# A two-layer encoder step on one core: in the RWKV-7 layer, values projected with tokens on the partitions, and a scan whose state is summed in PSUM and written by ScalarE

## The chip, the cores and the metric

One core of a Trainium2 chip runs the whole program. The metric is device time in microseconds (us), here of three runs, and of one more execution under the hardware profiler. The engines are TensorE (PE), VectorE (DVE), ScalarE (ACT), GpSimd (POOL) and SyncE (SP, which issues the DMAs).

## The reference

Two layers, each `x + Mixer(RMSNorm(x))`, on 2048 prompt tokens and 8 x 16 sample tokens of 1024 channels. Layer 1 is a gated DeltaNet; the change is in layer 2, RWKV-7, with 16 heads of 64 channels:

```python
rkvz = einsum('gbtd,dge->gbte', xs[:4], w_in)          # r, k, v, z: 1024 -> 4 x 1024
kk = l2_normalize(k * k_k);  k = k * (1 + (a - 1) * k_a)
def step(S, inp):                                       # S: one 64 x 64 state for each head
    sa = einsum('bhvk,bhk->bhv', S, a_t)
    S = S * w_t + sa * b_t + v_t * k_t
    return S, einsum('bhvk,bhk->bhv', S, r_t)
S, o = lax.scan(step, s0, (r, decay, k, v, -kk, kk * a))
o = group_norm(o) * gn_w + gn_b                         # by head
o = o + sum(r * k * r_k) * v                            # the bonus
y = (o * silu(z)) @ w_out
```

## The kernel before

The 2176 tokens of layer 2 run in six blocks: the first has two prompt chunks of 64 tokens and the 128 sample tokens (256 columns), the other five have six prompt chunks (384 columns). In a block the channels run in eight pairs of heads, q = 0..7, 128 channels each, so there are 48 steps of some 40 us. A step weaves, in twelve rounds, six stages of six successive pairs (`b_prep`, `b_subst`, `b_inverse`, the scan, `b_gate`, `b_out`) with 17 pieces of the projections of what comes next (`b_stream`). The order of TensorE is the written one; on the other engines and in SP's DMA queue a scheduler sorts by due times, DMAs with a lead of their own.

- **Projections** (`b_stream`, L1062 to L1064): 128x128 weights stationary, the mixed tokens `xh`, `xl` (high and low halves, made by `b_lerp` and L162/L163) moving with 384 columns, three matmuls for a product: 48 for a pair and group. `b_keep` copies the result with channels on the partitions to `kvo` (ACT) and writes it to DRAM (`kvd`); `b_load` reads K, R and V back.
- **`b_prep`**: products on POOL (L1181) and DVE; norm sums `pn`, twelve one-column matmuls (L1188); the bonus, one matmul with a block of ones over `rk` (L1198) into `pbn`, multiplied by V on DVE (L1200); Gram matrices (L1211), `N` (L1225, one half on DVE, one on POOL), then by DMA through DRAM `scrb` (L1236) into `B` (L1238).
- **`b_subst`**: a chain of small DVE operations L844/L846 on `B`, then by DMA into `cm`.
- **`b_inverse`**: POOL spreads `cm` into `T` (L1268), TensorE inverts by blocks (L1284 on), and twelve transposes (L106) turn V, which ACT copies into `XV` (L1327).
- **The scan**: a chunk is two rounds. First `px` (L1382) from `XV`, two ACT copies (L1385, L1386) and `Sw` = decay x state on ACT (L1384). In the second round KR·S (L1389) and TM·XV (L1393, into `pu`), then three DVE operations: the next chunk's `XV` twice (L1395) and the state `R` (L1396), each `pu` x decay + `Sw`; then L1398. There are 256 chunks in all.
- **`b_gate`, `b_out`**: normalise, turn back (L106), two fused DVE operations (L1485 and the next line) for weight, bonus, bias and gate, split into `oh`, `ol` (L163), output projection (L168 to L170).

A write of `whl` (L125) splits raw weights; `whl<-wd` loads split ones again. The functions that the change touches:

Of the kernel before, what the change touches and what calls it, by code (L numbers as in the profile page):

```python
# [29 lines left out]
NCI, NXH, NOH, NKO = 2, 8, 2, 2  # L30
# [41 lines left out]
class _K:  # L72
# [829 lines left out]
    def b_setup_side(self):  # L902

        nc, io, bp = self.nc, self.io, self.sp
        self.nacc, self.weng = 3, nc.vector
# [123 lines left out]
    def b_stream(self, blocks):  # L1029
# [17 lines left out]
        for b, units in pairs:  # L1047
            NT, first = b["NT"], units[0]
            if first == (1, 0):
                b["kv"] = self.dram.tile([4, KT, P, NT], F32, name=self.nm("kvd"), tag="kvd", bufs=2)  # L1050
# [4 lines left out]
            for s in range(4):
                for j, (g, q) in enumerate(units):
                    wh, wl = next(W)
                    o = p[j][:, 0:NT]
                    for i in range(2):
# [5 lines left out]
                    if s == 3:  # L1065
                        self.b_keep(b, g, q, p[j])
# [4 lines left out]
                    yield  # L1071

# [31 lines left out]
    def b_prep(self, b, q):  # L1104
# [88 lines left out]
        nc.vector.tensor_scalar(m2[:, 1, 0:nq], m2[:, 0, 0:nq], -1.0, None, op0=MUL)  # L1193
        yield
# [35 lines left out]
        d.update(KR=KR, BK=BK, m2=m2, bv=bv, GM=GM, N=N)  # L1230
# [24 lines left out]
    def b_inverse(self, b, q):  # L1255
# [3 lines left out]
        N, BK, V, GM = d["N"], d["BK"], d["V"], d["GM"]  # L1259
# [97 lines left out]
    def b_scan(self, b, q):  # L1357
# [19 lines left out]
        for c in range(ncp):  # L1377
# [5 lines left out]
            Sw = self.lp.tile([P, 64], F32, name=self.nm("Sw"), tag="Sw", bufs=2)  # L1383
            nc.scalar.activation(Sw, S, AF.Copy, scale=wc)  # L1384
# [78 lines left out]
    def b_gate(self, b, q):  # L1463
# [12 lines left out]
        nc.gpsimd.tensor_tensor(OC, OC, g[:, 0, 0:nq].unsqueeze(2).to_broadcast([P, nq, 64]), op=MUL)  # L1476
        yield
# [49 lines left out]
def _prep(inp):  # L1527
# [34 lines left out]
    o["b_prm"] = prm  # L1562
    w2 = np.stack([f["b_w_w2"][0], f["b_a_w2"][0]]).reshape(2, 64, KT, P).transpose(2, 1, 0, 3)
# [108 lines left out]
```

## Time and profile before

| what | value |
|---|---|
| median of three runs | 4623.11 us (4621.35 to 4625.97) |
| profiled execution | 4610.68 us, span 4608.9 us |
| busy in the span | PE 4299.8 (93%), DVE 3470.3 (75%), ACT 2287.8 (50%), POOL 1749.9 (38%) us |
| mean granted clock of TensorE | 0.966 |
| DMA | 842.18 MB, 183 GB/s |

Layer 2 begins near 2420 us of the span. Busy time is the union of an engine's instructions; a row of a timeline gives start and length, and in brackets the idle time ahead of it and what ended that. The granted clock is a share of full speed, 0.50 being the lower of the two levels. Times of the steps below are against the profiled execution, which stands 12.4 us (0.27%) under the median of the runs.

### The profile page before, as it was taken

To read this page: it belongs to the slowest core of one execution; us is meant where nothing else is said; L and a number is where in the kernel's file an instruction comes from. 1 tells how busy PE (TensorE), PEld (TensorE's weight loads), DVE (VectorE), ACT (ScalarE), POOL (GpSimd) and SP (SyncE) were. 2 spreads that over 40 slices of the span, in tenths; PEclk is the share of its full clock that TensorE was granted. 3 is DMA by queue.
4 is the path that set the end of the run, shared out by engine and by line. 5 is a ranking of instruction groups with operands and counts; after the bars stand their busy time and mean duration, and the time that the engine had idled before them with its cause. 6 is when DMAs were issued, how large, how long until landed. Compare 5 with 4: busy or idle time off the path is not lost. (4 is left out here: it accounts for less than half of the span.)

```text
span 4608.9 us, 104071 instructions
## 1 busy us (share of the span) xinstructions
PE 4299.8 (93%) x37093; PEld 3697.1 (80%) x37093; DVE 3470.3 (75%) x9203; ACT 2287.8 (50%) x6132; POOL 1749.9 (38%) x2507
## 2 busy tenths in 40 slices
PE   7999999999999999999987889999999999999996
PEld 6888788888888899999986767778787887887775
DVE  7888776676666776766677888877778778777885
ACT  5554454454344434444466665655455446446543
POOL 7666543322111211112103555445444434344441
PEclk9999999999999999999998989999999999999997
DMA  6666665556445576666655667766675665665542
GB/s 192 210 202 207 211 208 172 174 187 192 142 140 159 174 212 186 183 213 188 179 159 175 206 196 229 223 179 196 191 203 166 197 206 163 201 195 146 145 129 72
DMA packets 765670, 842.18 MB, mean 183 GB/s; under 512 B 263480, under 2 KB 497360, under 8 KB 765152
## 3 DMA queue, kind: packets, MB, share of 16 engines
q1 hardware_dynamic: 765152, 835.53, 59.9%
q8 instruction: 294, 4.82, 0.4%
q14 instruction: 224, 1.84, 0.1%
HBM read 632.73 MB, written 202.53 MB: 181 GB/s over the span
## 5 line engine op out<-in xcount | busy, mean ns | idle before, releaser
L453 PE MATMUL ps<-hh,whl 128*128 128x384 f32 (+1 forms) x1960 | 795.3, 406 | 12.8 <-ACT hh L162 10.6
L455 PE MATMUL ps<-hh,whl 128*128 128x384 f32 (+1 forms) x1960 | 711.8, 363 | 6.9 <-POOL whl L125 6.7
L454 PE MATMUL ps<-hl,whl 128*128 128x384 f32 (+1 forms) x1960 | 710.9, 363 | 1.7 <-DVE hl L163 1.4
L1062 PE MATMUL ps<-xh,whl 128*128 128x384 f32 (+1 forms) x1632 | 605.3, 371 | 32.0 <-ACT xh L162 17.4
L1063 PE MATMUL ps<-xl,whl 128*128 128x384 f32 (+1 forms) x1632 | 557.8, 342 | 22.0 <-POOL xl L163 11.2
L1064 PE MATMUL ps<-xh,whl 128*128 128x384 f32 (+1 forms) x1632 | 556.8, 341 | 9.2 <-DVE whl L125 8.8
L125 POOL TENSOR_TENSOR whl<-wraw,whl 128x256 fp32r<-128x256 f32 x454 | 374.6, 830 | 358.6 <-ACT whl L124 331.5
L573 DVE SCALAR_TENSOR_TENSOR cv<-pre,cw,cv 128x512 f32<-128x512 f32 (+3 forms) x576 | 375.3, 660 | 134.9 <-ACT cv L571 130.2
L453 PEld LDWEIGHTS ps<-hh,whl 128*128 128x128 f32 x1960 | 371.9, 190 | 65.8 <-issue 14.1
L168 PE MATMUL ps<-oh,whl 128*128 128x384 f32 (+2 forms) x1024 | 390.3, 381 | 26.6 <-DMA whl<-wd 13.9
L124 ACT CAST whl<-wraw 128x256 fp32r<-128x256 f32 x726 | 287.2, 402 | 255.5 <-DMA wraw<-in_w_b 74.3
L455 PEld LDWEIGHTS ps<-hh,whl 128*128 128x128 f32 x1960 | 371.4, 189 | 48.2 <-POOL whl L125 12.7
L454 PEld LDWEIGHTS ps<-hl,whl 128*128 128x128 f32 x1960 | 372.7, 190 | 34.0 <-DVE hl L163 4.6
L1062 PEld LDWEIGHTS ps<-xh,whl 128*128 128x128 f32 x1632 | 320.7, 197 | 75.3 <-ACT xh L162 23.0
L169 PE MATMUL ps<-ol,whl 128*128 128x384 f32 (+2 forms) x1024 | 366.8, 358 | 7.6 <-DVE ol L163 7.6
L844 DVE TENSOR_TENSOR sbt<-B,TB 48x15 f32<-48x15 f32 (+14 forms) x1320 | 351.9, 267 | 22.3 <-DMA B<-scr 1.7
L170 PE MATMUL ps<-oh,whl 128*128 128x384 f32 (+2 forms) x1024 | 363.6, 355 | 1.8 <-POOL whl L125 1.8
L846 DVE TENSOR_TENSOR TB<-TB,sbt 48x15 f32<-48x15 f32 (+14 forms) x1320 | 348.9, 264 | 19.8
L1063 PEld LDWEIGHTS ps<-xl,whl 128*128 128x128 f32 x1632 | 322.5, 198 | 33.8 <-POOL xl L163 17.2
L1064 PEld LDWEIGHTS ps<-xh,whl 128*128 128x128 f32 x1632 | 321.7, 197 | 16.8 <-DVE whl L125 16.2
L822 DVE TENSOR_TENSOR x<-x,ps 128x384 f32<-128x384 f32 (+1 forms) x320 | 191.1, 597 | 79.4 <-PE ps L170 77.9
L168 PEld LDWEIGHTS ps<-oh,whl 128*128 128x128 f32 x1024 | 196.6, 192 | 66.1 <-ACT oh L162 10.7
(349 smaller groups left out, 10233.7 us busy)
## 6 DMA issues: line engine op xcount, KB each, us to landing
whl<-wd SPq DMA_DIRECT2D x1582, 256.0 KB
wd<-whl SPq DMA_DIRECT2D x428, 256.0 KB
wraw<-in_w_a SPq DMA_DIRECT2D x288, 128.0 KB
wraw<-in_w_b SPq DMA_DIRECT2D x256, 128.0 KB
kvd<-kvo SPq DMA_DIRECT2D x160, 192.0 KB
xn<-x1d SPq DMA_DIRECT2D x80, 192.0 KB
wraw<-in_w_ao SPq DMA_DIRECT2D x96, 128.0 KB
xn<-in_x SPq DMA_DIRECT2D x32, 256.0 KB
```

What stands on the lines that cost most here:

```text
L125: (self.nc.gpsimd if tag == "o" else self.weng).tensor_tensor(w[:, 1], raw, w[:, 0].bitcast(F32), op=SUB)
L168: self.nc.tensor.matmul(out, lhsT=wh, rhs=hh, start=first and i == 0, stop=False)
L169: self.nc.tensor.matmul(out, lhsT=wh, rhs=hl, start=False, stop=False)
L170: self.nc.tensor.matmul(out, lhsT=wl, rhs=hh, start=False, stop=i == n - 1)
L453: nc.tensor.matmul(p, lhsT=wh[:, k % 2], rhs=hh, start=k == 0, stop=False)
L454: nc.tensor.matmul(p, lhsT=wh[:, k % 2], rhs=hl, start=False, stop=False)
L455: nc.tensor.matmul(p, lhsT=wl[:, k % 2], rhs=hh, start=False, stop=k == KT - 1)
L573: nc.vector.scalar_tensor_tensor(o, f(j), self.cw[:, ct, j:j + 1], o, op0=MUL, op1=ADD)
L844: nc.vector.tensor_tensor(o, B[:, j + 1:16, j:j + 1].to_broadcast([rows, m, j + 1]), T[:, j:j + 1, 0:j + 1].to_broadcast([rows, m, j + 1]) ...
L1062: nc.tensor.matmul(o, lhsT=wh[:, i], rhs=xh, start=k == 0, stop=False)
L1063: nc.tensor.matmul(o, lhsT=wh[:, i], rhs=xl, start=False, stop=False)
L1064: nc.tensor.matmul(o, lhsT=wl[:, i], rhs=xh, start=False, stop=k == KT - 1)
```

## The change

Three things in layer 2. **Values with tokens on the partitions:** `b_values` makes the tokens stationary (128 at a time, L1093 to L1095 of the new code) and moves 256 columns of weights, for two pairs at once; a matmul with a zero operand opens the bank that two token tiles share (L1090). `b_keep_values` makes three ACT copies for two pairs, and `XV` is loaded by DMA in `b_inverse` (L1316), so V isn't loaded, turned or copied. **The bonus by token:** the sum of `rk` is twelve one-column matmuls (L1225) right behind `pn`, two rounds earlier than the old matmul; POOL makes `bv` = `XV` x sum (L1364), and the gate adds it ahead of the turn, with the norm's weight from a broadcast tile. **The scan:** the state enters `pu` by a matmul with the identity (L1430), so `pu` x decay is the new state; ACT writes it (L1435 twice, L1436), and `Sw` goes.

```diff
-NCI, NXH, NOH, NKO = 2, 8, 2, 2
+NCI, NXH, NOH, NKO = 2, 8, 2, 3
...
+                    if g == 2:
+                        self.b_values(b, 2 * s + j, wh, wl, p)
+                        if s == 3 and j:
+                            self.b_keep_values(b, first[1], p)
...
+        if k == 0:
+            self.nc.tensor.matmul(p[0], lhsT=self.zero.to_broadcast([P, P]), rhs=wh.unsqueeze(1).to_broadcast([P, 2, 256]), start=True, stop=False)
+        for t in range(b["NT"] // P):
+            o, ts = p[t // 2][:, t % 2 * 256:t % 2 * 256 + 256], slice(t * P, (t + 1) * P)
+            self.nc.tensor.matmul(o, lhsT=xh[:, ts], rhs=wh, start=k == 0 and t == 2, stop=False)
...
+        for t in range(b["NT"] // P):
+            v = self.sp.tile([P, 256], F32, name=self.nm("kvo"), tag="kvo", bufs=NKO)
+            self.nc.scalar.copy(v, p[t // 2][:, t % 2 * 256:t % 2 * 256 + 256])
+            self.nc.sync.dma_start(b["vt"][t * P:(t + 1) * P, q * P:q * P + 256], v)
...
+        pb = self.ps("g")
+        for c in range(nq):
+            for h, hs in enumerate(HS):
+                nc.tensor.matmul(pb[HS[1 - h], c:c + 1], lhsT=c3(rk)[hs, c], rhs=self.ones[hs, 0:1], start=True, stop=True,
+                                 tile_position=(64 * h, 64 - 64 * h))
...
-        pbn = self.ps("g")
-        nc.tensor.matmul(pbn[:, 0:NT], lhsT=cb[:, B_BO:B_BO + P], rhs=rk, start=True, stop=True)
-        bv = self.lp.tile([P, NT], F32, name=self.nm("bv"), tag="bv", bufs=4)
-        nc.vector.tensor_tensor(bv, pbn[:, 0:NT], V, op=MUL)
+        bs = self.mp.tile([P, 8], F32, name=self.nm("bs"), tag="bs", bufs=3)
+        nc.scalar.activation(bs[:, 0:nq], pb[:, 0:nq], AF.Copy, scale=0.5)
...
+            nc.sync.dma_start(XV[os, 0:nq, h], vt[:, :, vs])
...
-        pt = self.ps("g")
-        for c in range(nq):
-            for h, hs in enumerate(HS):
-                self.turn(pt[HS[1 - h], c * 64:(c + 1) * 64], c3(V)[hs, c], h, 1 - h)
...
-            nc.scalar.copy(XV[os, 0:nq, h], c3(pt[os, 0:nq * 64]))
+            nc.gpsimd.tensor_tensor(bv[os], XV[os, 0:nq, h], d["bs"][os, 0:nq].unsqueeze(2).to_broadcast([64, nq, 64]), op=MUL)
...
-            Sw = self.lp.tile([P, 64], F32, name=self.nm("Sw"), tag="Sw", bufs=2)
-            nc.scalar.activation(Sw, S, AF.Copy, scale=wc)
...
+                nc.tensor.matmul(pu[HS[h], 0:64], lhsT=self.ident[HS[h], HS[h]], rhs=S[HS[h]], start=True, stop=False,
+                                 tile_position=(64 * h, 64 * h))
...
-                nc.vector.scalar_tensor_tensor(XV[HS[h], c + 1, h], pu[HS[h], 0:64], wc[HS[h]], Sw[HS[h]], op0=MUL, op1=ADD)
-            nc.vector.scalar_tensor_tensor(S, pu[:, 0:64], wc, Sw, op0=MUL, op1=ADD)
+                nc.scalar.activation(XV[HS[h], c + 1, h], pu[HS[h], 0:64], AF.Copy, scale=wc[HS[h]])
+            nc.scalar.activation(S, pu[:, 0:64], AF.Copy, scale=wc)
...
+        nc.vector.tensor_tensor(OC, OC, self.gw[:, q:q + 1].to_broadcast([P, nq, 64]), op=MUL)
+        nc.vector.tensor_tensor(OC, OC, d["bv"], op=ADD)
...
-        nc.vector.scalar_tensor_tensor(og, pu[:, 0:NT], self.hp[:, q, 3:4], og, op0=MUL, op1=ADD)
-        nc.vector.scalar_tensor_tensor(og, og, self.hp[:, q, 4:5], SZ, op0=ADD, op1=MUL)
+        nc.vector.scalar_tensor_tensor(og, pu[:, 0:NT], self.hp[:, q, 4:5], SZ, op0=ADD, op1=MUL)
```

**TensorE, a step in a six-chunk block, before:** the second half of a scan chunk, projections, the matmul of the bonus, and `px` of the next chunk. A name is a buffer with its number; `x2` are the two heads.

```order
L1389 MATMUL ps_46696<-R_30377,KR_44648 64x64 x2
L1393 MATMUL ps_46994<-XV_45920,TM_45919 64x64 x2
L1398 MATMUL ps_46696<-XV_45920,GM_45017 64x64 x2
L1062 MATMUL ps_46756<-xh_46431,whl_46835 128x384
L1063 MATMUL ps_46756<-xl_46432,whl_46835 128x384
L1064 MATMUL ps_46756<-xh_46431,whl_46835 128x384
L1062 MATMUL ps_46756<-xh_46438,whl_46835 128x384
L1063 MATMUL ps_46756<-xl_46439,whl_46835 128x384
L1064 MATMUL ps_46756<-xh_46438,whl_46835 128x384
L1198 MATMUL ps_47013<-ch_46784,cb 128x384
L1382 MATMUL ps_47023<-XV_45920,GM_45017 64x64 x2
```

After, the second half of a chunk:

```order
L1425 MATMUL ps_46159<-R_30380,KR_44236 64x64 x2
L1430 MATMUL ps_46870<-R_30380,ident 64x64 x2
L1433 MATMUL ps_46870<-XV_45490,TM_45489 64x64 x2
L1438 MATMUL ps_46159<-XV_45490,GM_44572 64x64 x2
L168 MATMUL ps_46885<-oh_45814,whl_46837 128x384
```

and the place where `pn` stands in a step of a block of the same kind, between two pieces of the values:

```order
L1093 MATMUL ps_47049<-whl_46912,xh_46568 128x256
L1094 MATMUL ps_47049<-whl_46912,xl_46569 128x256
L1095 MATMUL ps_47049<-whl_46912,xh_46568 128x256
L1219 MATMUL ps_47195<-ones,ch_47078 64x1 x12
L1225 MATMUL ps_47208<-ones,ch_47080 64x1 x12
L1420 MATMUL ps_47236<-XV_46120,GM_45279 64x64 x2
L1093 MATMUL ps_47048<-whl_46989,xh_46679 128x256
```

The bonus matmul is gone from the place ahead of `px`, its twelve small ones stand behind `pn`, and the identity's pair stands between KR·S and TM·XV.

**ScalarE, before, around one chunk:** `Sw`, a cast of mixed tokens, `XV` of the next pair, and the two copies of `px`.

```order
L1101 CAST w_11335_45847<-w2r_45845 128x256
L1384 ACTIVATE Sw_44815<-R_30371,wc_42563 128x64
L162 CAST xh_44626<-xt_44623 128x384
L1327 COPY XV_44575<-ps_44791 64x6x64
L1385 COPY XV_43907<-ps_44812 64x64
L1386 COPY XV_43907<-ps_44812 64x64
```

**ScalarE, after:** from a chunk's first `XV` write to its `R`.

```order
L1132 CAST w_11530_47587<-w2r_47585 128x256
L162 CAST xh_46238<-xt_46235 128x384
L162 CAST xh_46328<-xt_46325 128x384
L1435 ACTIVATE XV_45490<-ps_46376,wc_44221 64x64 x2
L1359 COPY Z_46125<-ps_46353 32x192 x2
L1018 ACTIVATE xt_46332<-H_42815,mu 128x384
L1018 ACTIVATE xt_46339<-H_42815,mu 128x384
L1421 COPY XV_45490<-ps_46435 64x64
L1422 COPY XV_45490<-ps_46435 64x64
L1436 ACTIVATE R_30380<-ps_46376,wc_44221 128x64
```

The write of the next `XV` (L1435) now stands on ScalarE, here behind two casts of mixed tokens (L162), whose `xt` DVE finishes; a cast stands between L1422 and L1435 in 56 of 215 chunks.

**SP's queue, before, around the load of B** (through DRAM `scrb`):

```order
L1236 DMA scrb_40956<-N_40951 64x6x64 x2
L133 DMA whl_40995<-wd_35189 128x512
L128 DMA wd_40977<-whl_40974 128x512
L133 DMA whl_41003<-wd_35202 128x512
L1238 DMA B_40959<-scrb_40956 48x16x16
L1089 DMA kvd_37731<-kvo_41011 128x384
```

**After:**

```order
L1271 DMA scrb_41119<-N_41114 64x6x64
L133 DMA whl_41160<-wd_35231 128x512
L1271 DMA scrb_41119<-N_41114 64x6x64
L128 DMA wd_41142<-whl_41139 128x512
L1316 DMA XV_41201<-vtd_32024 64x6x64
L133 DMA whl_41171<-wd_35247 128x512
L1273 DMA B_41122<-scrb_41119 48x16x16
L133 DMA whl_41248<-wd_35316 128x512
L1316 DMA XV_41201<-vtd_32024 64x6x64
```

The loads of `XV` are new in the queue, and one of them stands ahead of B's load; so it does in about half of the steps. The load of `XV` writes a buffer (of two) that the scan of two pairs before has read.

## Rows read from the trace of the kernel before

**Rows 1.** Windows, layer 2: us, busy us of PE, PEld, DVE, ACT, POOL; PEclk
```profile
2420.00:4609.00 2189.00, 1973.73 (x22757) 1661.00 (x22755) 1724.50 (x4691) 1152.92 (x3183) 982.48 (x1261) 0.94 0.60 180
```

**Rows 2.** PE's waits in layer 2: us in total, times, longest
```profile
PE ps L1382 <- DVE XV L1395: 43.5, 39, 2.6
PE ps L1284 <- POOL T L1268: 17.0, 5, 7.3
PE ps L1062 <- ACT xh L162: 16.9, 15, 2.2
...
PE ps L1064 <- DVE whl L125: 8.3, 15, 1.2
PE ps L169 <- DVE ol L163: 7.6, 19, 0.7
```

**Rows 3.** Timeline, PE, one such wait: start us, length us, line
```profile
3735.19 0.80 PE L1382 MATMUL ps<-XV,GM 128*64 128x64 f32 x4 [2.25 <-DVE XV L1395]
```

**Rows 4.** Timeline, DVE in the stretch before it
```profile
3728.99 0.99 DVE L844 TENSOR_TENSOR sbt<-B,TB 48x48 f32<-48x48 f32 x1
...
3732.68 0.20 DVE L844 TENSOR_TENSOR sbt<-B,TB 48x55 f32<-48x55 f32 x1
```

**Rows 5.** Timeline, POOL in the same stretch
```profile
3725.84 6.33 POOL L1181 TENSOR_TENSOR BK<-ch,ch 64x384 f32<-64x384 f32 x4
```

**Rows 6.** Timeline, ACT in the same stretch
```profile
3732.78 1.17 ACT L162 CAST xh<-xt 128x384 fp32r<-128x384 f32 x2 [2.31 <-DVE xt L1012]
```

**Rows 7.** Windows, twelve stretches that begin at such a wait: one, and the sum
```profile
3735.20:3738.60 3.40, 3.40 (x11) 2.76 (x12) 3.34 (x10) 1.18 (x4) 0.00 (x0) 0.51 0.21 70
...
sum 54.40, PE 51.34 PEld 43.61 DVE 44.31 ACT 20.49 POOL 3.75; mean PE 4.28 PEld 3.63 DVE 3.69 ACT 1.71 POOL 0.31
```

**Rows 8.** Groups of DVE in layer 2: count, busy us, mean ns, idle before
```profile
L1395 DVE SCALAR_TENSOR_TENSOR XV<-ps,wc,Sw 64x64 f32<-64x64 f32 x416 | 116.7, 281 | 82.2 <-PE ps L1393 71.7 <-PE ps L1398 2.7
...
L1200 DVE TENSOR_TENSOR bv<-ps,V 128x384 f32<-128x384 f32 x40 | 22.2, 554 | 0.7
```

**Rows 9.** Timeline, PE around the matmul of the bonus
```profile
3424.15 0.81 PE L1198 MATMUL ps<-ch,cb 128*128 128x384 f32 x2
3424.89 0.34 PE L1382 MATMUL ps<-XV,GM 128*64 128x64 f32 x4
```

**Rows 10.** Timeline, PE, eleven projection matmuls of 384 columns, first and last
```profile
3009.57 0.34 PE L1062 MATMUL ps<-xh,whl 128*128 128x384 f32 x1
...
3011.33 0.34 PE L1063 MATMUL ps<-xl,whl 128*128 128x384 f32 x1
```

**Rows 11.** Timeline, PE, eleven projection matmuls of 256 columns, first and last
```profile
2408.82 0.28 PE L1062 MATMUL ps<-xh,whl 128*128 128x256 f32 x1
...
2410.01 0.28 PE L1063 MATMUL ps<-xl,whl 128*128 128x256 f32 x1
```

**Rows 12.** Timeline, PE, norm sums, then turns of V: first, and the next line
```profile
3549.37 0.69 PE L1188 MATMUL ps<-ones,ch 64*64 64x1 f32 x18
...
3550.71 0.34 PE L1382 MATMUL ps<-XV,GM 128*64 128x64 f32 x4
```

**Rows 13.** Timeline, PE, second half of a chunk
```profile
3312.84 0.33 PE L1389 MATMUL ps<-R,KR 64*64 64x64 f32 x4
3313.11 0.34 PE L1393 MATMUL ps<-XV,TM 128*64 128x64 f32 x4
```

**Rows 14.** Groups of ACT in layer 2
```profile
L1384 ACT ACTIVATE Sw<-R,wc 128x64 f32<-128x64 f32 x256 | 85.0, 346 | 153.7 <-DVE R L1396 147.5 <-DVE TB L846 3.2 <-DVE sbt L844 1.0
...
L1385 ACT COPY XV<-ps 64x64 f32<-64x64 f32 x256 | 52.5, 205 | 110.5 <-PE ps L1382 108.0
```

**Rows 15.** Groups of POOL in layer 2
```profile
L1268 POOL TENSOR_TENSOR T<-cm,cb 128x384 f32<-128x384 f32 x80 | 67.8, 855 | 124.5 <-DMA cm<-sc2b 78.4 <-PE ps L1348 34.3 <-PE ps L170 5.7
...
L1225 POOL TENSOR_TENSOR N<-GM,m 64x384 f32<-64x384 f32 x40 | 39.9, 998 | 83.0 <-issue 41.0 <-DVE GM L1216 39.8 <-POOL T L1268 1.0
```

**Rows 16.** The tile scrb: issues on SP, ns min/median/max
```profile
L1236 SPq DMA_DIRECT2D scrb<-N x93: 574/581/1375, 2500.2 to 4499.4; - x93
```

More of the change, by code (lines that the diff above doesn't have):

```diff
@@ L908, in b_setup_side @@
         nc.vector.tensor_scalar(mu[:, 1], mu[:, 0], -1.0, 1.0, op0=MUL, op1=ADD)
+        self.zero = bp.tile([P, 1], F32R, name="zero")
+        nc.gpsimd.memset(self.zero.bitcast(F32), 0.0)
         hc = bp.tile([P, KT, 1], F32, name="hc")
@@ L922, in b_setup @@
         nc.vector.tensor_scalar(hp[:, :, 5:6], hp[:, :, 2:3], -1.0, 1.0, op0=MUL, op1=ADD)
+        gw = bp.tile([P, KT, 64], F32, name="gw")
+        for h in range(2):
+            nc.sync.dma_start(gw[64 - 64 * h:P - 64 * h].rearrange("p q v -> p (q v)"), io["b_gw"][h, :].partition_broadcast(64))
+        nc.vector.tensor_scalar(gw, gw, 0.5, None, op0=MUL)
+        self.gw = gw
         sm = bp.tile([P, NB], F32, name="smb")
@@ L1057, in b_stream @@
                     wh, wl = next(W)
+                    if g == 2:
+                        self.b_values(b, 2 * s + j, wh, wl, p)
+                        if s == 3 and j:
+                            self.b_keep_values(b, first[1], p)
                     o = p[j][:, 0:NT]
-                    for i in range(2):
+                    for i in range(2 if g != 2 else 0):
                         k = 2 * s + i
@@ L1064, in b_stream @@
                         nc.tensor.matmul(o, lhsT=wl[:, i], rhs=xh, start=False, stop=k == KT - 1)
-                    if s == 3:
+                    if s == 3 and g != 2:
                         self.b_keep(b, g, q, p[j])
@@ L1071, in b_stream, with b_values, b_keep_values @@
                     yield
+    def b_values(self, b, k, wh, wl, p):
+        xh, xl = b["X", 2, k]
+        wh, wl = [w.rearrange("p j c -> p (j c)") for w in (wh, wl)]
+        if k == 0:
[3 more added lines that the diff above has]
+            self.nc.tensor.matmul(o, lhsT=xh[:, ts], rhs=wh, start=k == 0 and t == 2, stop=False)
+            self.nc.tensor.matmul(o, lhsT=xl[:, ts], rhs=wh, start=False, stop=False)
+            self.nc.tensor.matmul(o, lhsT=xh[:, ts], rhs=wl, start=False, stop=k == KT - 1 and t > 0)
+    def b_keep_values(self, b, q, p):
+        for t in range(b["NT"] // P):
+            v = self.sp.tile([P, 256], F32, name=self.nm("kvo"), tag="kvo", bufs=NKO)
+            self.nc.scalar.copy(v, p[t // 2][:, t % 2 * 256:t % 2 * 256 + 256])
+            self.nc.sync.dma_start(b["vt"][t * P:(t + 1) * P, q * P:q * P + 256], v)
+        b.setdefault("kept", set()).update({(2, q), (2, q + 1)})
     def b_keep(self, b, g, q, p):
@@ L1229, in b_prep @@
                 nc.gpsimd.memset(GM[hs, ncp:nq, h, 0:64], 0.0)
-        d.update(KR=KR, BK=BK, m2=m2, bv=bv, GM=GM, N=N)
+        d.update(KR=KR, BK=BK, m2=m2, GM=GM, N=N)
         nb = nq * 8
@@ L1271, in b_inverse @@
         T, Tt = Ts
+        ex = 2 * b["nsc"]
+        TM = self.lp.tile([P, nq + ex, 2, 64], F32, name=self.nm("TM"), tag="TM", bufs=2)
+        XV = self.lp.tile([P, nq + ex, 2, 64], F32, name=self.nm("XV"), tag="XV", bufs=2)
+        VS = self.lp.tile([P, 2 * ex, 64], F32, name=self.nm("VS"), tag="VS", bufs=2) if ex else None
+        assert (2, q) in b["kept"]
+        vt = b["vt"].rearrange("(c t) x -> t c x", t=64)
+        for h in range(2):
+            os, vs = HS[1 - h], slice(q * P + 64 * h, q * P + 64 * h + 64)
+            nc.sync.dma_start(XV[os, 0:nq, h], vt[:, :, vs])
+            if ex:
+                nc.sync.dma_start(VS[os, 0:ex], vt[:, ncp:nq, vs])
         N16 = self.lp.tile([P, ncp, 64], F32, name=self.nm("N16"), tag="ci", bufs=NCI)
@@ L1392, in b_scan @@
             for h in range(2):
-                nc.tensor.matmul(pu[HS[h], 0:64], lhsT=TM[:, c, h], rhs=XV[:, c, h], start=True, stop=True, tile_position=(0, 64 * h))
+                nc.tensor.matmul(pu[HS[h], 0:64], lhsT=self.ident[HS[h], HS[h]], rhs=S[HS[h]], start=True, stop=False,
+                                 tile_position=(64 * h, 64 * h))
+            for h in range(2):
+                nc.tensor.matmul(pu[HS[h], 0:64], lhsT=TM[:, c, h], rhs=XV[:, c, h], start=False, stop=True, tile_position=(0, 64 * h))
             for h in range(2 if c + 1 < ncp else 0):
-                nc.vector.scalar_tensor_tensor(XV[HS[h], c + 1, h], pu[HS[h], 0:64], wc[HS[h]], Sw[HS[h]], op0=MUL, op1=ADD)
-            nc.vector.scalar_tensor_tensor(S, pu[:, 0:64], wc, Sw, op0=MUL, op1=ADD)
+                nc.scalar.activation(XV[HS[h], c + 1, h], pu[HS[h], 0:64], AF.Copy, scale=wc[HS[h]])
+            nc.scalar.activation(S, pu[:, 0:64], AF.Copy, scale=wc)
             for h in range(2):
```

21 lines of the change are left out of this document (10 added, 11 removed).

## The prediction, made before the changed kernel had run

> **What bounds the kernel now.** I read the windows first: in layer 2 TensorE is busy for 1973.73 of 2189 us, DVE for 1724.50, ScalarE for 1152.92, POOL for 982.48 [rows 1]. TensorE is the bound, so the edit can pay in two ways: fewer or shorter matmuls, or shorter waits of TensorE. Its list of waits comes next [rows 2]. The longest entry is the first matmul of a scan chunk, L1382, which waits for DVE's write of `XV` (L1395): 43.5 us in 39 waits out of 256 chunks. The reader is to see that the other 217 chunks don't wait; the round trip of a chunk is hidden most of the time.
>
> A timeline shows why the 39 are late. In one of them L1382 stands 2.25 us [rows 3]. In the stretch before it DVE works off small operations of the substitution, and one of the same shape takes 0.99 us where a later one takes 0.20 [rows 4]; beside the slow one POOL runs a string of 64x384 products for 6.33 us [rows 5]. DVE falls behind, and the update of `XV`, one of its queue, with it. ScalarE stands idle beside it for 2.31 us, but what it waits for is itself a product of DVE (`xt`) [rows 6]. Then the granted clock: twelve stretches that begin at such a wait run at the lower level, 54.40 us together [rows 7]. At half speed they cost 54.40 / 2 = 27 us more than the same work at full clock.
>
> **The change part by part.** All sums are against the profiled execution; at the end I add the 12.4 us by which the median of the runs stands over it.
>
> *The bonus matmul.* From its start to the next matmul's it takes 0.74 us [rows 9]. Without it, `px` enters straight behind a projection, which I put 0.1 dearer than behind the bonus: -0.64 x 40 pairs, and some -0.3 x 8 for the short block: -28 us. The twelve small matmuls in its place stand in the string with `pn`, where before it the twelve turns of V stood. These 24 took 1.34 us [rows 12], or 0.056 each, and there are 24 again: 0. Should the turns have been dearer than one-column matmuls, up to 0.3 a step or 14 us more comes off.
>
> *The values.* Eleven matmuls of 384 columns start within 1.76 us, 0.176 apart [rows 10]; of 256 columns within 1.19 us, 0.119 apart [rows 11]. Two pairs took 2 x 8 x 3 = 48 matmuls of 384: 8.45 us. They take 8 x 3 x 3 = 72 of 256, and the opening one of 512, which by the same slope is 0.233: 8.80 us. +0.35 x 20 = 7, and in the short block +0.23 x 4 = 1: +8 us. Both banks now end with the last piece, so the next projection needs ScalarE's copies at once, where before one bank was free a piece earlier. I price that with the wait of L1062 for ScalarE, 16.9 / 15 = 1.1 us [rows 2], at a third of the 24 places: +9 us; ends 0 (the scan's matmuls stand between) and 26.
>
> *The identity matmuls.* 256 chunks get two more. Such matmuls follow each other at 0.056 in a string [rows 12], which gives 256 x 0.11 = 28 us; alone, a pair takes 0.27 to the next line [rows 13], 69 us; if it hides in the time that TM·XV takes to enter, 0. They stand right behind a pair of the same shape, so I take the string: +28 us.
>
> *The wait for `XV`.* DVE loses 416 updates at 281 ns, 116.7 us [rows 8], 256 of `R` at the same price, 72, the bonus product, 40 x 554 ns = 22 [rows 8], and one of two fused operations of the gate, about 22; it gains two products in the gate, 80 x 0.55 = 44. Net -189 us, 9% of layer 2. ScalarE gains the 672 updates at 346 ns, the price of `Sw`, which has the same form, and loses `Sw`, 85.0 [rows 14]: +147 us at most, to 59% of layer 2. The update on ScalarE is 65 ns longer than on DVE, but in 217 chunks there is cover for that. In ScalarE's queue it stands behind casts whose input DVE makes, in about a quarter of the chunks, so some of DVE's lateness stays in the path. I take 60% of the 43.5 us: -26, ends 0 and -43.5. The clock follows the waits: 60% of 27, -16, ends 0 and -27.
>
> *Other waits for DVE.* L1064 for `whl` and L169 for `ol`, 8.3 and 7.6 us [rows 2]: with DVE relieved I take two thirds, -10; ends 0 and -16.
>
> *POOL.* `bv` is 80 products at 998 ns [rows 15], +80 us on 982, where only `T` has anyone waiting: TensorE waits for it 17.0 us in five steps [rows 2]. POOL itself stood 78.4 us for `cm` ahead of it [rows 15], so `bv` falls beside idle time: 0.
>
> The row beside a running POOL product, 0.99 against 0.20 [rows 4], has a rule: the Trainium skill (SBUF — State Buffer, Who interferes with whom) says that a DVE operation with two SBUF inputs contends with a GpSimd instruction that reads SBUF, one of them locked out. The trace agrees in direction, and the rule speaks against `bv` on POOL: 80 us more of it could take back up to 80 of the 189 us, and the sum would lose 4 of the last 10.
>
> *Tail.* Past the last projection nothing covers a chunk; six chunks with two updates 0.065 longer are 0.8 us, and the gate's two products against one fused operation less add some 0.6 on two pairs: +3 us with the new load.
>
> Sum: -28 + 8 + 9 + 28 - 26 - 16 - 10 + 3 = **-32 us**: 4578.7 for an execution like the profiled one, **4591 us** on the scale of the median.
>
> **The rivals.**
>
> *A: all of it goes through.* DVE's lateness leaves the scan entirely and the identity's pair hides in the entry of TM·XV. For it: ScalarE is at 53%, and L1393 isn't in the list of long waits although it waits for ScalarE's copies. Against: ScalarE waits for DVE itself [rows 6]. -28 + 8 + 9 - 43.5 - 27 - 16 + 3 = -95: 4529 us.
>
> *B: the wait stays and changes its name.* L1420 waits for ScalarE, held by casts that wait for DVE, or `pb` waits for `rk`, needed two rounds earlier. For it: the 2.31 us of [rows 6] fall in the very stretch in which L1382 waits. Against: a quarter of the chunks have the cast ahead, and these aren't the same as the late ones. Without the 26 and the 16 the sum is +10, or about 4633, on the bound of what counts as no change; with the values' evacuation at its lower end 4624. Beside it stands the Trainium skill (ScalarE: Activation LUTs, Rules for kernel authors), which gives plain multiplies to VectorE; its figures for a pointer operand (What ACT_TABLE_LOAD costs) make 332 ns as an estimate, and the trace has 346 against DVE's 281 [rows 14, 8]. Were all 256 chunks bound by their round trip, two writes at 65 ns would be 33 us, and the sum 0.
>
> *C: slower, SP's queue.* The loads of `XV` stand ahead of B's in half of the steps and each issue costs 0.58 us [rows 16]; moreover they can't go before the scan of two pairs earlier has read the buffer, and what is behind them waits too. B late makes `cm` late, and with it `T`, for which TensorE already waits 3.4 us (17.0 / 5) in five steps [rows 2]. For it: POOL waits for `cm` 78.4 us in all, so `T` has no reserve of its own [rows 15]. Against: relieved by 9%, DVE ends the substitution earlier. It decides once B comes later by more than that gains, 189 / 48 = 3.9 us a step at most; two issues alone are 1.2. If twenty more steps wait, that is 20 x 3.4 = 68 us, and if each wait is followed by a stretch at the lower clock as in [rows 7] (54.40 / 12 / 2 = 2.3 us each), 45 more: -32 + 113 = +81, 4704 us; with ten steps, 4648.
>
> That the change wouldn't do what it says is no case: the orders show `Sw`, the turns and the matmul gone.
>
> **How the numbers follow.** Forecast 0.50, A 0.15, B 0.18, C 0.17. What a measurement of this kernel can tell from no change is 0.2%, 9.2 us: 4613.9 to 4632.4. The forecast's own range, with the identity's pair at 0.27 us less half of A's gains at one end, is 4550 to 4630, so that some 0.44 of its 0.50 is faster by more than that bound. Faster: 0.44 + 0.15 + 0.03 of B = 0.62. Same: 0.05 + 0.12 + 0.03 of C = 0.20. Slower: 0.01 + 0.03 + 0.14 = 0.18. The range leaves out the far half of A and most of C: 4525 to 4645.
>
> **What would show it.** Right, in the changed kernel's profile: L1420 waits some 17 us for ScalarE instead of 43.5 for DVE; DVE's busy time in layer 2 near 1535 us, ScalarE's below 1300; TensorE at its second half of a chunk 0.1 us longer; no line for the bonus; the mean clock of layer 2 above 0.94. Wrong: L1420 waiting 40 us or more (B); `T` waited for in fifteen or more steps, or the loads of `XV` long in SP's list of waits (C); the pair with the identity taking over 0.2 us; projections behind the values standing for ScalarE by more than 1.1 us each.

## The result and the profile after

The changed kernel takes 4746.47 us, median of four runs (4745.11 to 4749.08), beside 4624.54 for the kernel before in the same comparison: ratio 1.0262, 95% interval 1.0240 to 1.0284. It is slower by 2.6%, some 122 us, where 4591 was forecast and 4645 was the upper end. The profiled execution's span is 4747.4 us. Below, times taken from ratios are against 4624 us.

The window of layer 2 answers to [rows 1], in the same columns:

```profile
2420.00:4747.00 2327.00, 2029.07 (x24259) 1748.59 (x24257) 1664.36 (x4059) 1244.40 (x3602) 1064.43 (x1359) 0.90 0.58 171
```

Layer 2 is 138 us longer. POOL is busy for 82 us more, as worked out, and ScalarE for 92 more, below the 147 that were the most. DVE isn't where it was expected: 60 us less, where 189 less, near 1535, was forecast. TensorE's time divides so. Its list of waits adds up to 289 us, where all of the list before adds up to 203: +86. The granted clock is 0.90 where it was 0.94; as a share of the window that is 0.10 x 2327 = 233 us lost at the lower level, before 0.06 x 2189 = 131: +102, good to some 20 us with clocks of two digits. What is left, TensorE's own work at full clock, fell by about 50. Some waits lie in stretches at the lower level and are counted twice in this; taken from TensorE's busy time and the clock's record, the parts are +83 for idle time (298 us, before 215), +86 for the clock (half of 389 us of work at the lower level, before of 216) and -31 for the work. So the matmuls' own time was not the loss; stalls and the lower clock were. The list of waits after:

```profile
PE ps L1355 <- DVE T L1349: 47.4, 26, 3.7
PE ps L1420 <- ACT XV L1435: 24.4, 19, 3.5
...
PE ps L1225 <- DVE ch L1194: 17.2, 10, 3.5
...
PE ps L1331 <- POOL T L1303: 12.9, 3, 8.3
```

The chunk's first matmul (now L1420) waits less than in [rows 2], for ScalarE. But a product of the inverse that waits for DVE's `T` (L1349) now waits 47.4 us, 26 times, and the sum of `rk` (L1225) 17.2 us. In the kernel before, the product's wait was

```profile
PE ps L1313 <- DVE T L1307: 2.3, 5, 0.5
```

One such step, on TensorE:

```profile
3770.89 0.34 PE L1076 MATMUL ps<-xh,whl 128*128 128x384 f32 x1
3774.93 0.80 PE L1355 MATMUL ps<-T,N 32*32 32x32 f32 x22 [3.71 <-DVE T L1349]
```

on DVE in the stretch before (start, length, line, idle time ahead in brackets):

```profile
3762.68 1.36 DVE L1517 TENSOR_TENSOR OC<-OC,gw 128x384 f32<-128x384 f32 x1 [2.14 <-POOL OC L1516]
...
3765.07 1.36 DVE L1518 TENSOR_TENSOR OC<-OC,bv 128x384 f32<-128x384 f32 x1
...
3769.13 0.73 DVE L844 TENSOR_TENSOR sbt<-B,TB 48x15 f32<-48x15 f32 x1
3769.90 0.18 DVE L846 TENSOR_TENSOR TB<-TB,sbt 48x15 f32<-48x15 f32 x1
...
3771.34 0.20 DVE L844 TENSOR_TENSOR sbt<-B,TB 48x48 f32<-48x48 f32 x1
...
3771.80 0.96 DVE L844 TENSOR_TENSOR sbt<-B,TB 48x55 f32<-48x55 f32 x1
3772.80 1.05 DVE L846 TENSOR_TENSOR TB<-TB,sbt 48x55 f32<-48x55 f32 x1
...
3774.25 0.54 DVE L1349 TENSOR_TENSOR T<-T,ps 128x384 f32<-128x384 f32 x1
```

and on POOL:

```profile
3763.71 1.02 POOL L1364 TENSOR_TENSOR bv<-XV,bs 64x384 f32<-64x384 f32 x1
...
3768.36 1.47 POOL L1364 TENSOR_TENSOR bv<-XV,bs 64x384 f32<-64x384 f32 x1
3771.77 0.93 POOL L1207 TENSOR_TENSOR KR<-ch,Ep 128x384 f32<-128x384 f32 x1 [1.94 <-DVE TB L846]
...
3772.79 0.99 POOL L1212 TENSOR_TENSOR BK<-ch,ch 64x384 f32<-64x384 f32 x1
```

The reader is to see three things: DVE stood for 2.14 us in front of the gate's product (L1517) until POOL had made `OC`; its two gate products took 1.36 us each; and a small operation of the substitution takes 0.73 beside POOL's second `bv` (L1364) and 0.18 behind it, 0.20 while POOL stands, and 0.96 beside POOL's next product (L1207), where one of this size took 0.20 in [rows 4]. `T` comes behind all of it. In the last microsecond of the wait the clock falls, and it stays at the lower level for 10 us:

```profile
3774.10:3784.40 10.30, 9.47 (x107) 8.63 (x108) 8.58 (x30) 2.62 (x9) 3.72 (x4) 0.50 0.55 168
```

Over all 48 steps the first of the three alone is, in DVE's list of waits,

```profile
DVE OC L1517 <- POOL OC L1516: 100.5, 48, 3.2
```

### The profile page after: what moved, and what is told of

Read it like the earlier page. It is cut to its first block, busy times and chain, and to the rows that moved or that the text cites. A ratio compares the mean times of both kernels' runs of the same rounds, so it can differ in the third digit from the quotient of the medians.

```text
span 4747.4 us, 106637 instructions
## 1 busy us (share of the span) xinstructions
PE 4359.1 (92%) x38525; PEld 3790.5 (80%) x38525; DVE 3398.2 (72%) x8532; ACT 2366.3 (50%) x6512; POOL 1828.7 (39%) x2604
## 4 chain that ended last, share of the span: by engine, by line
PE 57%; DVE 21%; DMA 6%; POOL 6%; issue 5%; ACT 4%; SPq 1%; POOLq 0%; ACTq 0%; DVEq 0%
PE ps L453 6%; PE ps L455 6%; PE ps L454 6%; PE ps L168 4%; PE ps L169 4%; PE ps L170 3%; PE ps L1074 3%; DVE sbt L844 3%; PE ps L1076 2%; PE ps L1075 2%; DVE TB L846 2%; DVE cv L573 1%; DMA wraw<-in_w_b 1%; DMA whl<-wd 1%; PE ps L1246 1%
## 5 line engine op out<-in xcount | busy, mean ns | idle before, releaser
L1074 PE MATMUL ps<-xh,whl 128*128 128x384 f32 (+1 forms) x1248 | 472.3, 378 | 36.9 <-DVE kvo L1119 18.6
L1076 PE MATMUL ps<-xh,whl 128*128 128x384 f32 (+1 forms) x1248 | 438.8, 352 | 11.7 <-DVE whl L125 11.3
L1075 PE MATMUL ps<-xl,whl 128*128 128x384 f32 (+1 forms) x1248 | 436.5, 350 | 12.9 <-POOL xl L163 8.8
L844 DVE TENSOR_TENSOR sbt<-B,TB 48x15 f32<-48x15 f32 (+14 forms) x1320 | 371.7, 282 | 25.3 <-DMA B<-scr 2.0
L1074 PEld LDWEIGHTS ps<-xh,whl 128*128 128x128 f32 x1248 | 252.5, 202 | 68.8 <-DVE kvo L1119 20.3
L1076 PEld LDWEIGHTS ps<-xh,whl 128*128 128x128 f32 x1248 | 254.7, 204 | 19.3 <-DVE whl L125 19.1
L1075 PEld LDWEIGHTS ps<-xl,whl 128*128 128x128 f32 x1248 | 255.3, 205 | 17.0 <-POOL xl L163 10.7
```

The source lines that it names most:

```text
L844: nc.vector.tensor_tensor(o, B[:, j + 1:16, j:j + 1].to_broadcast([rows, m, j + 1]), T[:, j:j + 1, 0:j + 1].to_broadcast([rows, m, j + 1]) ...
L1074: nc.tensor.matmul(o, lhsT=wh[:, i], rhs=xh, start=k == 0, stop=False)
L1075: nc.tensor.matmul(o, lhsT=wh[:, i], rhs=xl, start=False, stop=False)
L1076: nc.tensor.matmul(o, lhsT=wl[:, i], rhs=xh, start=False, stop=k == KT - 1)
```

## The experiments

Every ratio is to the kernel before, run on the same chip; intervals are 95%.

**Which half of the change.** `e1_values_only` is the changed kernel with the old scan, `e2_scan_only` the old kernel with the new scan:

```diff
 e1 (on the changed kernel; ... marks what is left out)
-                nc.tensor.matmul(pu[...], lhsT=self.ident[...], rhs=S[HS[h]], ...)
-                nc.scalar.activation(XV[HS[h], c + 1, h], pu[...], AF.Copy, scale=wc[HS[h]])
+                nc.vector.scalar_tensor_tensor(XV[HS[h], c + 1, h], pu[...], wc[HS[h]], Sw[HS[h]], op0=MUL, op1=ADD)
 ... (`Sw` and the write of `R` likewise)
 e2 (on the kernel before): the same lines the other way round
```

> The change with the scan of the kernel before: Sw on ScalarE, XV and R written by DVE, no identity matmuls; values, bonus and gate as changed. Theory 1 (DVE is held in the gate: the product with the norm's weight waits for POOL's product on the same tile, and the update T of the inverse is late behind it): this part alone is slower than before, 4680 to 4760 us, with DVE still some 100 us idle for POOL's OC and TensorE waiting 30 us or more for T. Theory 2 (the scan on ScalarE costs it: identity matmuls and late XV): 4600 to 4640 us, and T is waited for under 10 us.

> The kernel before with the scan alone changed: identity matmuls, XV and R written by ScalarE, Sw gone; values with channels on the partitions, the bonus matmul and the gate as before. Theory 1: 4590 to 4630 us, the first matmul of a chunk waiting some 20 us for ScalarE instead of 43.5 for DVE, T waited for under 10 us. Theory 2: 4680 us or more. The identity's pair at 0.11 us a chunk would be 28 us, at 0.27 69 us.

Measured: e1 4751.81 us, 1.0267 (1.0236 to 1.0297); e2 4620.23 us, 0.9978 (0.9962 to 0.9995). The scan isn't the loss; by itself it gains 0.22%. `T` is waited for 13.7 us there, a little over the 10 that theory 1 allowed. The wait of e2 for `XV`, and its window:

```profile
PE ps L1382 <- ACT XV L1396: 18.1, 19, 2.4
```

```profile
2420.00:4628.00 2208.00, 1979.35 (x23875) 1675.29 (x23875) 1606.08 (x4067) 1280.10 (x3648) 973.75 (x1263) 0.95 0.61 180
```

In e1 DVE waits 103.9 us for POOL's OC, as theory 1 had it, but its lateness shows at `XV`, which DVE writes again (57.5 us), and `T` is waited for 12.4 us, not 30. The time is the same as that of the changed kernel.

**The gate, and the sum's place.** `e3_gate_on_pool` puts the gate's two products on POOL, `e4_bonus_two_rounds_later` the twelve matmuls where the old one stood:

```diff
 e3
-        nc.vector.tensor_tensor(OC, OC, self.gw[...], op=MUL)
-        nc.vector.tensor_tensor(OC, OC, d["bv"], op=ADD)
+        nc.gpsimd.tensor_tensor(OC, OC, self.gw[...], op=MUL)
+        nc.gpsimd.tensor_tensor(OC, OC, d["bv"], op=ADD)
 e4 (in words)
-        pb matmuls, bs copy
         yield
         yield
+        pb matmuls, bs copy
```

> The changed kernel with the gate's two products (norm's weight, bonus) on POOL instead of DVE, so that DVE waits for POOL's OC no more. Theory 1: the 100 us of idle DVE go, T is waited for 15 us at most, and the time falls to 4640 to 4690 us. Theory 3 (T is late because the sum of rk is needed two rounds earlier, which puts b_prep's DVE work and the substitution ahead of T in DVE's queue): T is still waited for 35 us or more, 4725 to 4760 us.

> The changed kernel with the twelve bonus matmuls and their copy two rounds later, where the old bonus matmul stood. Theory 1: the wait of TensorE for rk (17.2 us) goes, the wait for T stays at 35 us or more, 4715 to 4745 us. Theory 3: T is waited for 15 us at most, 4640 to 4690 us.

Measured: e3 4758.48 us, 1.0273 (1.0247 to 1.0299), `T` waited for 38.9 us; e4 4741.34, 1.0243 (1.0212 to 1.0273), `T` 42.4 us. Both theories fell as they stood: theory 1 in e3, where DVE no longer waits for POOL in the gate and `T` is late all the same, theory 3 in e4, where TensorE's wait for `rk` is gone and the wait for `T` stays. With the gate on POOL, POOL's string is longer, and two small operations of DVE in a row are slow beside it:

```profile
4072.38 0.93 DVE L844 TENSOR_TENSOR sbt<-B,TB 48x39 f32<-48x39 f32 x1
4073.35 1.03 DVE L846 TENSOR_TENSOR TB<-TB,sbt 48x39 f32<-48x39 f32 x1
4074.42 0.20 DVE L844 TENSOR_TENSOR sbt<-B,TB 48x48 f32<-48x48 f32 x1
```

**Values or bonus.** `e5_no_bonus` takes all of the bonus out of the changed kernel; `e6_token_bonus_old_values` puts the bonus by token on the old values, with the scan of e2.

> The changed kernel with the bonus left out of the computation (no matmuls for the sum of rk, no bv on POOL, no products in the gate before the turn; norm's weight and bias and the gate in two DVE operations after the turn, as many as before): the values with tokens on the partitions, the loads of XV and the scan on ScalarE stay. Theory 4 (the bonus by token costs it: POOL's bv beside DVE, and the gate's two products on DVE behind POOL's): 4580 to 4630 us, T waited for under 15 us. Theory 5 (the values cost it: their matmuls, banks and loads): 4690 us or more.

> The kernel before with the scan on ScalarE and the bonus by token (one-column matmuls, bv on POOL from XV, two products in the gate), but the values projected with channels on the partitions, loaded and turned as before. The gate takes the norm's weights of the first pair for all pairs. Theory 4: 4700 us or more. Theory 5: 4600 to 4640 us.

Measured: e5 4601.19 us, 0.9963 (0.9945 to 0.9981), `T` waited for 15.8 us; e6 4740.34, 1.0257 (1.0232 to 1.0282). The whole loss is the bonus by token; how the values are projected and loaded makes no difference that can be seen (e6 against the changed kernel, 1.0257 and 1.0262).

**DVE's load and order.** `e7_bv_on_dve` changes one word (`nc.gpsimd` to `nc.vector` at `bv`). `e8_t_ahead_of_substitution` holds the substitution by a copy from `T` of the inverse (`held`):

```diff
+            if j == 2 and hold:
+                nc.vector.tensor_copy(tmp[0:1, 0:1], self.held[0:1, 0, 0:1])
...
-                parts.append((self.b_subst(*at(i - 1)), range(1, 9)))
+                parts.append((self.b_subst(*at(i - 1)), range(2, 10)))
```

> The changed kernel with the product bv on DVE instead of POOL. If POOL's string, two products longer, holds DVE (theory 4a): T is waited for 25 us or less and the time is 4680 to 4720 us, although DVE has 1 us more a step to do. If not: 4740 us or more.

> The changed kernel with the order of DVE's queue as before at one place: a one-element copy that reads T holds the substitution at four operations until T is written, where 8 to 14 stood ahead of T in every second step; the substitution starts one round later. If that order is the cause (theory 6: DVE's order, made for a DVE that isn't held up by POOL, puts the substitution ahead of T): T waited for under 15 us and 4640 to 4690 us. If DVE is late in any case: the waits move to XV, to cm or to other products of DVE, and the time is 4720 us or more.

Measured: e7 4709.12 us, 1.0189 (1.0165 to 1.0213), the time that theory 4a gave, with `T` waited for 28.6 us where it had 25 at most; e8 4724.72, 1.0229 (1.0199 to 1.0260). In e8 the wait for `T` fell as it should, to

```profile
PE ps L1358 <- DVE T L1351: 16.3, 16, 2.4
```

but the time by 0.33% only, with overlapping intervals: the wait for `T` is 31 us shorter, all waits of TensorE together 15 (289 to 274), so about half of what `T` gained came back in other waits.

**The bonus in its parts.** Three kernels on the changed one: `e9_sum_only` keeps of the bonus the twelve matmuls and ScalarE's copy, `e10_sum_and_bv` POOL's `bv` as well, `e11_gate_products_only` the gate's products alone.

> The changed kernel with only the sum of rk of its bonus left (twelve one-column matmuls and ScalarE's small copy, two rounds earlier than the old bonus matmul); bv and the gate's products before the turn are left out, so the bonus isn't added. Theory 4b (the early sum costs it: TensorE waits for rk and runs a longer string of one-column matmuls): 4670 us or more. Theory 4c (the gate's two products): 4600 to 4640 us, as without the bonus or up to 30 us more.

> The changed kernel with the sum of rk and POOL's bv, but without the gate's two products before the turn (the bonus is made and not added). Against the run with the sum alone it prices bv on POOL. Theory 4a (bv): 35 to 60 us above that run. Theory 4c: within 20 us of it.

> The changed kernel with the gate's two products before the turn, but without the sum of rk and without bv (the second product adds the norm's weights once more in place of the bonus). Theory 4c (DVE waits 2.1 us for POOL in each step and works 2 us beside it): 4660 to 4720 us, T waited for 25 us or more. Theories 4a and 4b: 4600 to 4640 us.

| kernel | time, us | ratio | interval |
|---|---|---|---|
| no bonus (e5) | 4601.19 | 0.9963 | 0.9945 to 0.9981 |
| sum (e9) | 4646.91 | 1.0036 | 1.0021 to 1.0050 |
| sum, bv (e10) | 4714.68 | 1.0184 | 1.0159 to 1.0208 |
| sum, bv, gate (the change) | 4746.47 | 1.0262 | 1.0240 to 1.0284 |
| gate (e11) | 4649.81 | 1.0042 | 1.0024 to 1.0060 |

So the sum costs 0.73%, 34 us; `bv` 1.48%, 68 us; the gate's products 0.78% behind the other two and 0.79% alone, 36 us; each difference is good to 0.2 or 0.3%. None of the three theories had it alone: e9 and e11 stand between the two ranges that were expected of each, `bv` a little above its 35 to 60 us. The parts add up. Windows of e5, e9, e10 and e11, in this order:

```profile
2420.00:4591.00 2171.00, 1941.94 (x23130) 1658.24 (x23128) 1586.92 (x3990) 1227.85 (x3533) 998.30 (x1262) 0.93 0.62 182
```

```profile
2420.00:4650.00 2230.00, 2007.71 (x24247) 1728.69 (x24245) 1584.61 (x4005) 1241.65 (x3596) 972.66 (x1263) 0.91 0.62 178
```

```profile
2420.00:4710.00 2290.00, 2034.91 (x24241) 1752.70 (x24239) 1621.80 (x4002) 1240.28 (x3593) 1060.87 (x1359) 0.90 0.60 173
```

```profile
2420.00:4639.00 2219.00, 1978.18 (x23133) 1687.62 (x23132) 1602.45 (x4040) 1229.42 (x3535) 995.03 (x1263) 0.92 0.62 179
```

From e5 to e9 DVE does no more and TensorE's waits add up to 7 us less (219 and 213); twelve more matmuls a step are there, and the clock falls from 0.93 to 0.91, which is 0.09 x 2230 - 0.07 x 2171 = 49 us. Over all ten runs of each, the mean granted clock of the whole program is 0.959 in e5 and 0.952 in e9, where the kernel before has 0.963; 0.007 of 4620 us is 32. In e9 the waits are

```profile
PE ps L1225 <- DVE ch L1194: 14.3, 13, 3.9
PE ps L1355 <- DVE T L1349: 14.2, 11, 2.2
```

and in the clock's record eleven stretches at the lower level, 58 us together, begin within 2.6 us of the end of a wait at L1225, seven of them behind a wait of only 0.4 us; in nine of the eleven the one-column matmuls had ended before the clock fell. Part of the 34 us is plainer: it is the time of the twelve matmuls. The string in e5 and in e9, at full clock, each with the matmul behind it:

```profile
3420.27 0.86 PE L1219 MATMUL ps<-ones,ch 64*64 64x1 f32 x24
3421.06 0.34 PE L1406 MATMUL ps<-XV,GM 128*64 128x64 f32 x4
```

```profile
3401.82 0.69 PE L1219 MATMUL ps<-ones,ch 64*64 64x1 f32 x18
...
3403.12 0.34 PE L1415 MATMUL ps<-XV,GM 128*64 128x64 f32 x4
```

That is 0.79 us and 1.30, so 0.51 a step and some 20 us in 40 steps. From e9 to e10 DVE's busy time grows by 37 us (1584.61 to 1621.80), though it has nothing more to do, and the wait for `T` doubles:

```profile
PE ps L1355 <- DVE T L1349: 30.3, 15, 3.5
```

**Place or work.** Each part moved: `e12_bv_behind_t3` puts `bv` behind POOL's last product on `T`, `e13_gate_products_behind_t` the gate's products behind `T` on DVE, `e14_all_three_moved` both, and the sum two rounds later.

```diff
 e12
+        nc.gpsimd.tensor_copy(bs2[:, 0:1], T3[:, 0, 0:1])
+        nc.gpsimd.tensor_copy(bs2[:, 0:nq], d["bs"][:, 0:nq])
 ... (then bv as before, from bs2)
 e13 (two yields later)
+        nc.vector.tensor_scalar(hd, self.held[:, 0, 0:1], 0.0, None, op0=MUL)
+        nc.vector.scalar_tensor_tensor(OC, OC, hd, self.gw[...], op0=ADD, op1=MUL)
+        nc.vector.tensor_tensor(OC, OC, d["bv"], op=ADD)
```

> The changed kernel with POOL's bv moved: it now stands behind POOL's last product on T in the same step (a copy of the sums that reads T first holds it there), where POOL otherwise waits for cm, instead of in the string of products beside DVE's substitution. If the place is the cause: 40 to 70 us less than the changed kernel, 4680 to 4705 us, and T waited for under 30 us. If the two products as such are: within 20 us of it.

> The changed kernel with the gate's two products moved two rounds later and held behind T on DVE (the first reads a zero made from T). If DVE's wait for POOL ahead of T is the cause: DVE's idle time for POOL's OC falls from 100 to under 20 us and the time by 25 to 45 us, to 4700 to 4720 us. If the products' work is: within 15 us of the changed kernel.

> The changed kernel with all three moved: the sum of rk two rounds later, bv behind T's last product on POOL, the gate's products behind T on DVE. If the places are the cause: 4620 to 4660 us, near the kernel without the bonus plus 16 us for twelve matmuls a step and some 10 for the rest. If the work is: 4700 us or more.

Measured: e12 4749.29 us, 1.0241 (1.0218 to 1.0264); e13 4721.02, 1.0174 (1.0145 to 1.0203); e14 4678.06, 1.0098 (1.0061 to 1.0136). For the gate the place, with its wait, is the cause: 0.88% comes back, and DVE's wait for POOL's OC falls from 100.5 us to

```profile
DVE OC L1522 <- POOL OC L1517: 16.8, 9, 3.1
```

For `bv` the place alone isn't: in e12 `T` is waited for 30.5 us instead of 47.4, and the time stays. All three together give back 1.64%, 76 us of 138, so e14 came out between its two expectations. From e13 to e14 that is 0.76% more, with intervals that don't overlap; whether `bv`'s place or the sum's brings it, once the gate's products are out of the way, no run separates.

**What of bv is it.** `e16_pool_busy_without_reading` is e10 with `bv`'s products replaced by a six-column copy from `XV` and two clears each, so that POOL is held as long, in the same place, with hardly a read:

```diff
-            nc.gpsimd.tensor_tensor(bv[os], XV[os, 0:nq, h], d["bs"][...].to_broadcast([64, nq, 64]), op=MUL)
+            nc.gpsimd.tensor_copy(bv[os, 0, 0:nq], XV[os, 0, h, 0:nq])
+            nc.gpsimd.memset(bv[os], 0.0)
+            nc.gpsimd.memset(bv[os], 0.0)
```

> The kernel with the sum and bv but no gate products, with bv's two products replaced on POOL by a six-column copy from XV and two clears of the same tile each (about 0.11 + 2 x 0.42 = 0.95 us for a product of 1.03), in the same place of the queue; the bonus isn't made. If DVE's loss beside the reading product is the cause of the 68 us: within 20 us of the kernel with the sum alone (ratio 1.004 to 1.008). If POOL's own time is: within 20 us of the kernel with sum and bv (1.014 to 1.023).

Measured: 4652.56 us, 1.0041 (1.0024 to 1.0059): the 68 us are gone. POOL's groups, first of e10, then of e16, and e16's window:

```profile
L1364 POOL TENSOR_TENSOR bv<-XV,bs 64x384 f32<-64x384 f32 x80 | 82.3, 1028 | 4.5 <-DMA XV<-vtd 0.4
```

```profile
L1366 POOL MEMSET bv<- 64x384 f32 x80 | 33.1, 414 | 4.5
...
L1364 POOL COPY bv<-XV 64x6 f32<-64x6 f32 x80 | 29.1, 363 | 4.3 <-DMA XV<-vtd 1.1
```

```profile
2420.00:4642.00 2222.00, 1994.95 (x24230) 1715.54 (x24228) 1586.27 (x3996) 1239.15 (x3588) 1083.29 (x1551) 0.92 0.62 179
```

The copy and the clears take 1.19 us, more than the 0.95 expected, so POOL is busy longer than in e10 (1083.29 against 1060.87); ahead of the place it stands as little in both (4.5 and 4.3 us), so a wait for the sums isn't the difference. DVE is busy 35 us less, and `T` is waited for

```profile
PE ps L1355 <- DVE T L1349: 16.5, 11, 2.8
```

So `bv` costs what DVE loses beside a product that reads, not POOL's time. How 37 us of DVE become 68 us of the kernel is read from the longer wait for `T` and the lower clock, and isn't tested by a run of its own. The Trainium skill (SBUF — State Buffer, Who interferes with whom) says that a DVE operation with two SBUF inputs contends with a GpSimd instruction that reads SBUF and not with one that only writes it; e10 against e16 agrees on both.

**A version that beats both.** `e15_scan_only_t_first` is e2 with the hold of e8, `e17_before_t_first` the kernel before with it.

> The kernel before with the scan on ScalarE alone, and the substitution held at four operations until T is written. T is waited for 13.7 us in 12 places without the hold; with it under 8. 4595 to 4620 us, 0.2 to 0.6% under the kernel before; if the hold makes cm late instead, 4625 us or more, with more than 20 us of waiting for POOL's T.

> The kernel before with the substitution held at four operations until T is written, and nothing else. T was waited for only 2.3 us there, so there is little to gain: 0.998 to 1.003 of the kernel before. If it gains as much as with the scan on ScalarE: 0.996 or less.

Measured: e15 4610.55 us, 0.9938 (0.9909 to 0.9967), the fastest kernel here that computes all; e17 4624.16, 0.9982 (0.9965 to 0.9999). What the hold adds to e2 (0.9978, 0.9962 to 0.9995) is inside the intervals. In e15 `T` is hardly waited for, and `cm` isn't late:

```profile
PE ps L1286 <- POOL T L1270: 15.8, 5, 6.0
...
PE ps L1316 <- DVE T L1309: 0.5, 2, 0.2
```

## Why the prediction was wrong, point by point

- **Two terms of the sum failed that stood at 0.** "`bv` falls beside idle time: 0" looked at POOL's idle time alone: 68 us. For the gate's products I counted 44 us of DVE work and no wait; that the change itself makes DVE wait for POOL, 100.5 us, with `T` of the inverse queued behind, stands nowhere in the sum: 36 us. Their work was too small as well, 87 us instead of 44:

```profile
L1517 DVE TENSOR_TENSOR OC<-OC,gw 128x384 f32<-128x384 f32 (+1 forms) x48 | 45.3, 944 | 100.5 <-POOL OC L1516 100.5
L1518 DVE TENSOR_TENSOR OC<-OC,bv 128x384 f32<-128x384 f32 (+1 forms) x48 | 41.7, 870 | 1.0
```

- **The step of the twelve matmuls held.** "There are 24 again: 0": the string takes 1.30 us in e9 and took 1.34 before [rows 12]. The 34 us of the table stand against e5, which has neither the turns of V nor the small matmuls. The wait for `rk`, which I had named only inside rival B, came; with the sum two rounds later (e4) it is gone, and the time is the same within the intervals.
- **The third step that failed is "The clock follows the waits".** Without `bv` and the gate's products (e9) the change stands at 1.0036, +17 us, where -32 was forecast. With 68 and 36 these 49 us make up the whole miss. In e9 TensorE's waits are 10 us above those before (213 and 203), but the clock's share of the window is some 70 us above (0.09 x 2230 against 0.06 x 2189; over all runs 0.952 against 0.963, which is 51 us), where -16 was forecast. From e9 to the changed kernel it was the other way: waits +76, clock +32. Why the clock fell without longer waits stays open.
- **DVE's relief was a third of what was counted,** 60 us of 189. The gate's products took 43 us more than counted, and `bv` brought 37; and already in e2, which takes the same 189 us of updates off DVE, DVE is busy only 118 us less, so its other operations took 71 us more there. Why isn't shown.
- **The rule that spoke against the change was cited and priced too low:** "the sum would lose 4 of the last 10". DVE lost 37 us to `bv`, in line with "up to 80", but I let it weigh only on two small waits, not on `T`, `XV` and the clock.
- **The scan was right in kind.** L1420 waits 24.4 us and in e2 18.1, where 17 was forecast. The identity's pair: e2's window less its waits (218) and its clock's share (0.05 x 2208 = 110) leaves 1880 us of work, against 2189 - 203 - 131 = 1855 before: 25 us for a forecast of 28, good to some 20. The net gain of e2, 10 us, is under the 24 that its terms made (28 - 26 - 16 - 10): DVE's relief of other waits didn't come (7.7 us for `whl` and 8.2 for `ol` in e2, before 8.3 and 7.6). The term that the clock should give back with the shorter wait for `XV` came in this run: 0.967 against 0.963 over all runs, 16 us for a forecast of 16. An update on ScalarE takes 309 and 313 ns, not 346:

```profile
L1435 ACT ACTIVATE XV<-ps,wc 64x64 f32<-64x64 f32 x416 | 128.6, 309 | 42.1 <-PE ps L1433 33.2 <-PE ps L1438 1.7
...
L1436 ACT ACTIVATE R<-ps,wc 128x64 f32<-128x64 f32 x256 | 80.2, 313 | 50.7 <-PE ps L1433 44.8 <-PE ps L1438 0.6
```

- **The values can't be judged alone.** From e2 to e5 the forecast has +8 and +9 for them, -28 for the bonus matmul, and the turns of V go with nothing in their place, (1.34 - 0.79) x 40 = 22 us: -33. The time falls by 0.15%, 7 us, good to some 11. The mean clock fell between these two from 0.967 to 0.959, 35 us or so, while TensorE's waits stayed (218 and 219); an estimate from these numbers is that the work came off as priced and the lower clock took most of it back.
- **Rival C had the sign and not the mechanism.** Its 4704 was nearest, but `T` on POOL is waited for 12.9 us in three steps, less than in [rows 2]; no wait of TensorE names a load of `XV`, and POOL stood for one once, 7.9 us. The fifteen or more steps that wait for `T` came, as its sign said, but for DVE's `T`.

What stays open beside the clock: why e14 is still 62 us above the kernel without a bonus. The twelve matmuls' own time is some 20 of it; that `bv` still reads beside DVE is a likely part, but no run shows how much.

## What to carry to other kernels

When work moves to an engine "with idle time", ask what its reads do to the engine beside it, and what an in-order queue now waits for: here two products of 1.03 us a step on POOL and one new wait on DVE cost more than the matmul and the V path that they replaced saved. Price a new wait with what is queued behind it on its engine, not with the busy time of its instruction. Then ask for the clock by itself: in this kernel its share grew beside the stalls by about as much as they did, but not in step with them, and a forecast that let it follow the waits had its sign wrong.

## What the runs showed of the hardware that was not expected

POOL held twice a step for 1.19 us by a small copy and clears costs nothing that can be seen (e16 against e9, 1.0041 and 1.0036), and held as often for 1.03 us by a product that reads it costs 0.8 us of DVE time a step (37 us / 48) and 68 us in all. And the same twelve one-column matmuls moved the clock's mean of layer 2 from 0.93 to 0.91 while the waits of TensorE didn't grow (e5, e9).
